# Row-tiled attention scores, attention beside the down projections, and a new start order in an encoder block

## Chip, cores, metric

One Trainium2 chip, eight NeuronCores, one sequence of the batch on each. Time is device microseconds of the slowest core. Some executions fall in a slower state, in which the cores of one die (0 to 3 or 4 to 7) show a lower granted clock; only fast runs are compared here.

## The reference, cut to what matters

```python
x = x + 0.5 * swiglu(rmsnorm(x), ffn1...)            # 1024 -> 2816 -> 1024
h = rmsnorm(x);  z = h @ w_in                        # q, k, v, two SGU halves, gates
y_att = chunked_rel_attention(q, k, v, rel_bias)     # 8 heads of 64; 64-frame chunks see 9 chunks
y_sgu = spatial_gating(gelu(z_sgu))                  # 128-frame blocks
x = x + (sig(g_att) * (y_att @ w_a) + sig(g_sgu) * (y_sgu @ w_s)) @ w_out
x = x + 0.5 * swiglu(rmsnorm(x), ffn2...)
out = rmsnorm(x)                                     # (8, 4096, 1024) float32
```

## The kernel before

Frames go in eight tiles of 512. Attention of tile t runs beside dense work of another tile, in turns: `interleave(main, attention, ...)` takes a piece of each. A block of keys (128) and two heads make one step: two score matmuls, one exp, one multiplication by exp(bias), and two steps later two value matmuls. Each head's query is padded with zeros to 128 rows (QZ).

```python
def scores(i):
    for h in range(2):
        matmul(bank(4 + h)[:, 0:n], lhsT=KT[:, hp, kcol:kcol + 128], rhs=QZ[:, hp, h, q0:q0 + n])
    act.activation(out=ee, in_=PS[2][...], func=Exp)
    dve.tensor_tensor(out=ee, in0=ee, in1=EB[...], op=mult)
def pv(i):
    for h in range(2):
        matmul(bank(6 + h)[:, q0:q0 + n], lhsT=VR[...], rhs=E[:, i % 2, h, 0:n], start=first, stop=last)
    ...            # after the last block: four copies of sums and values (VectorE, ScalarE)
def recip(i, j):   # VectorE, in halves; the sums are also added up on GpSimd (OKA)
# main of tile 1 and later: the whole FFN, gate/up first
interleave(ffn(t + 1, 0, True, hooks), attention(t), N_FFN - 6, n_att(t), 6)
# start: tile 1 lags tile 0 by one chunk of gate/up weights (last chunk of tile 1 later)
for n, f2 in enumerate(F2J):
    gu_chunk(0, f2, slot, ...)
    if prev is not None: gu_chunk(1, F2J[n - 1], prev, ...)
```

## Time and profile before

| | before |
|---|---|
| median of three runs | 2804.32 us |
| profiled run, slowest core | 2803.8 us |
| mean granted clock of the cores | 0.991 to 0.994 |
| TensorE busy; its share of the chain | 97%; 92% |

The prediction shows the lines. In them PE is TensorE's matmuls, PEld its weight loads, DVE VectorE, ACT ScalarE, POOL GpSimd and SP SyncE; L812 is a line of the kernel, and `ps` is PSUM, in banks of 512 columns. One tool is used throughout, its "loss": the length of a stretch less the work that TensorE did in it, with each weight load at 0.216 us (512 columns), attention and mixing by their columns.

### The profile page before, as it was taken

To read this page: it belongs to the slowest core of one execution; us is meant where nothing else is said; L and a number is where in the kernel's file an instruction comes from. 1 tells how busy PE (TensorE), PEld (TensorE's weight loads), DVE (VectorE), ACT (ScalarE), POOL (GpSimd) and SP (SyncE) were. 2 spreads that over 40 slices of the span, in tenths; PEclk is the share of its full clock that TensorE was granted. 3 is DMA by queue.
4 is the path that set the end of the run, shared out by engine and by line. 5 is a ranking of instruction groups with operands and counts; after the bars stand their busy time and mean duration, and the time that the engine had idled before them with its cause. 6 is when DMAs were issued, how large, how long until landed. Compare 5 with 4: busy or idle time off the path is not lost.

```text
span 2803.8 us, 38175 instructions; the slowest of 8 cores (2798.0 to 2803.8 us)
## 1 busy us (share of the span) xinstructions
PE 2705.7 (97%) x12775; PEld 1246.5 (44%) x13034; DVE 1318.1 (47%) x2007; ACT 897.7 (32%) x1348; POOL 406.5 (14%) x426
## 2 busy tenths in 40 slices
PE   6999899999999999999999999999999999999997
PEld 2443344444444444444444444444444444444443
DVE  4553744374433743347433464425644265466432
ACT  3322333243322423224232332323333242433221
POOL 2001311202121011111111111110110102100111
PEclk9999999999999999999999999999999999999998
DMA  8879899986798555984444634446344444333451
GB/s 150 175 134 178 181 208 176 186 260 153 194 184 218 174 148 160 227 239 143 141 160 143 201 130 143 151 146 204 131 150 144 158 154 139 142 130 128 141 195 69
DMA packets 113111, 461.94 MB, mean 165 GB/s; under 512 B 9352, under 2 KB 12424, under 8 KB 104848
## 3 DMA queue, kind: packets, MB, share of 16 engines
q1 hardware_dynamic: 89600, 365.68, 39.3%
q0 software_dynamic: 23168, 93.69, 21.7%
q8 instruction: 112, 1.84, 0.3%
q14 instruction: 87, 0.71, 0.1%
q10 hardware_dynamic: 144, 0.02, 0.0%
HBM read 488.03 MB, written 65.01 MB: 197 GB/s over the span
## 4 chain that ended last, share of the span: by engine, by line
PE 92%; DVE 3%; issue 2%; ACT 1%; DMA 1%; DVEq 0%; POOL 0%; ACTq 0%; POOLq 0%
PE ps L560 41%; PE ps L626 21%; PE ps L930 8%; PE ps L677 6%; PE ps L690 4%; PE ps L940 4%; PE ps L959 4%; PE ps L821 2%; PE ps L807 2%; DMA RING<-fsrc 1%; DVE TG L831 0%; DVE TG L829 0%; PE ps L764 0%; PE ps L501 0%; DVE TG L944 0%
## 5 line engine op out<-in xcount | busy, mean ns | idle before, releaser
L560 PE MATMUL ps<-XT,RING 128*128 128x512 bf16 x5501 | 1258.5, 381 | 38.3 <-DMA RING<-fsrc 14.7
L560 PEld LDWEIGHTS ps<-XT,RING 128*128 128x128 bf16 x5632 | 546.9, 98 | 674.0 <-issue 51.6
L626 PE MATMUL ps<-HT,RING 128*128 128x512 bf16 x2603 | 579.5, 379 | 2.8
L584 DVE TENSOR_TENSOR HT<-ps,TG 128x512 bf16<-128x512 f32 x332 | 227.9, 687 | 368.6 <-PE ps L560 318.8
L626 PEld LDWEIGHTS ps<-HT,RING 128*128 128x128 bf16 x2656 | 259.0, 98 | 309.2 <-issue 1.8
L490 POOL TENSOR_TENSOR ACC<-ACC,TG 128x512 f32<-128x512 f32 x174 | 224.1, 1288 | 994.0 <-ACT TG L487 992.9
L487 ACT ACTIVATE TG<-X 128x512 f32<-128x512 f32 x224 | 140.1, 627 | 476.6 <-DVE X L632 405.7
L632 DVE SCALAR_TENSOR_TENSOR X<-ps,X 128x512 f32<-128x512 f32 x128 | 87.8, 687 | 328.4 <-PE ps L626 324.4
L930 PE MATMUL ps<-XT,RING 128*128 128x512 bf16 x1003 | 239.7, 379 | 0.9
L811 ACT ACTIVATE E<-ps 128x1024 bf16<-128x1024 f32 (+1 forms) x240 | 168.7, 703 | 204.6 <-PE ps L807 187.3
L573 ACT ACTIVATE TG<-ps 128x512 f32<-128x512 f32 x154 | 92.0, 597 | 372.9 <-PE ps L560 367.4
L814 DVE TENSOR_TENSOR E<-E,EB 128x1024 bf16<-128x1024 bf16 (+1 forms) x240 | 152.7, 637 | 78.9 <-ACT E L811 77.6
L839 POOL TENSOR_TENSOR OKA<-OKA,TG 128x512 f32<-128x512 f32 x64 | 85.5, 1336 | 662.2 <-DVE TG L829 458.0
L677 PE MATMUL ps<-XT,RING 128*128 128x512 bf16 x752 | 167.5, 379 | 0.8
L569 DVE SCALAR_TENSOR_TENSOR TG<-TG,ps 128x512 f32<-128x512 f32 x154 | 103.6, 673 | 121.8 <-ACT TG L567 105.2
L944 DVE SCALAR_TENSOR_TENSOR TG<-TG,ps 128x512 f32<-128x512 f32 x128 | 87.1, 685 | 153.9 <-PE ps L940 126.2
L935 ACT ACTIVATE TG<-ps,BG 128x512 f32<-128x512 f32 x128 | 87.3, 687 | 213.1 <-PE ps L930 206.5
L930 PEld LDWEIGHTS ps<-XT,RING 128*128 128x128 bf16 x1024 | 99.7, 98 | 120.8 <-issue 3.1
L567 ACT ACTIVATE TG<-ps 128x512 f32<-128x512 f32 x154 | 91.9, 597 | 186.2 <-PE ps L560 183.2
L512 DVE SCALAR_TENSOR_TENSOR XT<-X,G,RSTD 128x512 bf16<-128x512 f32 x176 | 124.5, 744 | 36.5 <-ACT RSTD L505 36.5
L847 DVE RECIPROCAL TG<-TG 128x256 f32<-128x256 f32 x64 | 111.7, 1746 | 24.6 <-POOL OKA L839 24.5
L690 PE MATMUL ps<-RING,XT 128*128 128x512 bf16 x501 | 117.2, 385 | 5.6 <-DVE XT L512 4.6
(102 smaller groups left out, 1773.1 us busy)
## 6 DMA issues: line engine op xcount, KB each, us to landing
RING<-ffs SPq DMA_DIRECT2D x126, 1024.0 KB, 6.1
RING<-wds SPq DMA_DIRECT2D x93, 704.0 KB, 4.7
RING<-fsrc POOLq DMA_DIRECT2D x38, 1024.0 KB, 15.6
RING<-mgs SPq DMA_DIRECT2D x48, 768.0 KB, 4.8
RING<-wis SPq DMA_DIRECT2D x32, 1024.0 KB, 6.0
RING<-wd POOLq DMA_DIRECT2D x35, 704.0 KB, 17.0
ffs<-RING SPq DMA_DIRECT2D x22, 1024.0 KB, 15.5
out<-X SPq DMA_DIRECT2D x32, 512.0 KB, 6.2
```

The costliest lines, as they stand in the source:

```text
L487: p.add("act", lambda e: e.activation(out=buf[:], in_=src, func=AF.Square, scale=1.0 / 32.0), reads=[xres], writes=[bres])
L490: p.add(eng, lambda e: e.tensor_tensor(out=ACC[:], in0=ACC[:], in1=buf[:], op=ALU.add), reads=["ACC", bres], writes=["ACC"])
L512: p.add("dve", lambda e: e.scalar_tensor_tensor(out=dst, in0=src, scalar=G4[:, which * 8 + d:which * 8 + d + 1], in1=RSTD[:], op0=ALU.mult ...
L560: p.add("pe", lambda e: e.matmul(bank(b), lhsT=Wc[:, j * 1024 + kc * 128:j * 1024 + (kc + 1) * 128], rhs=xt[:, kc, :], start=(kc == 0), st ...
L584: p.add("dve", lambda e: e.tensor_tensor(out=dst, in0=bank(bu), in1=buf[:], op=ALU.mult), reads=[rb(bu), bres], writes=[dres])
L626: p.add("pe", lambda e, fc=fc, W=W, by=by, hap=hap: e.matmul(bank(by), lhsT=W[:, fc * 128:(fc + 1) * 128], rhs=hap, start=(fc == 0), stop= ...
L677: p.add("pe", lambda e, kc=kc, W=W, b=b, cc=cc: e.matmul(bank(b), lhsT=W[:, kc * 512 + cc * 128:kc * 512 + (cc + 1) * 128], rhs=XT[t % 2][ ...
L690: p.add("pe", lambda e, kc=kc, W=W, b=b, s=s: e.matmul(bank(b), lhsT=XT[t % 2][:, kc, s * 128:(s + 1) * 128], rhs=W[:, kc * 512:(kc + 1) * ...
L811: p.add("act", lambda e: e.activation(out=ee, in_=PS[2][:].rearrange("p (h c) -> p h c", h=2)[:, :, 0:n], func=AF.Exp), reads=[rb(4), rb(5 ...
L814: p.add("dve", lambda e: e.tensor_tensor(out=ee, in0=ee, in1=EB[:, 2 * hp:2 * hp + 2, u0:u0 + n], op=ALU.mult), reads=[("E", i % 2), ("EB" ...
L930: p.add("pe", lambda e, kc=kc, W=W, bgt=bgt, j=j: e.matmul(bank(bgt), lhsT=W[:, j * 1024 + kc * 128:j * 1024 + (kc + 1) * 128], rhs=XT[t % ...
L940: p.add("pe", lambda e, c4=c4, W=W, bbr=bbr, j=j, Y=Y: e.matmul(bank(bbr), lhsT=W[:, 2048 + j * 512 + c4 * 128:2048 + j * 512 + (c4 + 1) * ...
```

## The change

Intent: halve the score matmuls by running two heads in two row halves of the array; put attention only beside down projections, where ScalarE and VectorE have little else; replace slow reciprocals by exp(-log); start faster. The diff, cut to its core (left out: names of other buffers, weight layout and first loads, memsets moved to GpSimd, eight PSUM banks in the first gate/up stage, the order of the two branches in the merge, the fallback path):

```diff
-        E = sb("E", [128, 2, 2, T], BF16)
+        E = sb("E", [128, 4, 2, T], BF16)
-    bank(4 + h)[:, 0:n], lhsT=KT[:, hp, kcol:kcol + 128], rhs=QZ[:, hp, h, q0:q0 + n]
+    hs = slice(h * 64, (h + 1) * 64)        # two blocks of keys in a step, four banks
+    bank(2 + 2 * j + h)[:, q0:q1], lhsT=KT[hs, hp, kcol:kcol + 128], rhs=Q[hs, hp, q0:q1]
-    p.add("dve", ... e.reciprocal(out=r2[:, sl], in_=r2[:, sl]))
+    p.add("act", ... e.activation(out=r2[vs, :], in_=bank(6 + h)[ds, :], func=AF.Ln))
+    p.add("act", ... e.activation(out=r2[:], in_=r2[:], func=AF.Exp, scale=-1.0, accum_out=col))
+    for s in range(N + 1):                  # values half a step later
+        if s < N: scores(s); weigh(); yield
+        if s: pv(s - 1); yield
 ...
+    if narrow and fc in (5, 16): yield      # down projection in quarter pieces, two banks
-    main = ffn(t + 1, 0, True, ffn1_hooks(t + 1))
-    interleave(main, attention(t), N_FFN - 6, n_att(t), 6)
+    main = ffn(t + 1, 0, True, ffn1_hooks(t + 1), narrow=True)
+    interleave(main, attention(t), N_FFN + 16 - 3, n_att(t), 2 * NFC)
 ...
-    if prev is not None: yield from gu_chunk(1, F2J[n - 1], prev, ...)
+    if n == 1: yield from gu_chunk(1, F2J[0], prev, ..., first=0)
+    if 0 < n < len(F2J) - 1: yield from gu_chunk(1, f2, slot, ..., first=n)
+    second = down(1, 0, 0.5, Hooks(hk), ht_second, narrow=1)
+    for _ in range(4): next(second)         # ahead of the input projection
     win(0, {})
```

## The prediction

> **What bounds the kernel now.** I read the page first, its busy line and the chain that ended last.
> ```profile
> PE 2705.7 (97%) x12775; PEld 1246.5 (44%) x13034; DVE 1318.1 (47%) x2007; ACT 897.7 (32%) x1348; POOL 406.5 (14%) x426
> PE 92%; DVE 3%; issue 2%; ACT 1%; DMA 1%; DVEq 0%; POOL 0%; ACTq 0%; POOLq 0%
> ```
> The chain is TensorE for 92% of the span; VectorE, the next, is busy for 47%. So time falls only if TensorE gets less work or loses fewer microseconds. A busy share of 97% does not tell these two apart, so I looked at the spacing of matmuls in the timeline (start, length, engine).
> ```profile
> 562.37 0.59 PE L807 MATMUL ps<-QZ,KT 128*128 128x512 bf16 x2
> ...
> 564.86 1.89 PE L560 MATMUL ps<-XT,RING 128*128 128x512 bf16 x8
> ```
> One matmul is shown 0.38 us long, but eight take 1.89, so they start (1.89 - 0.38) / 7 = 0.216 us apart, and the score pair, 0.59 - 0.38 = 0.21, too. That is the price of 512 columns; a weight load (98 ns) hides beside it.
>
> Work, from the kernel's loops: a tile of 512 frames has 1056 matmuls in the two FFNs, 160 in the input projection and 256 in the merge, 1472 in all; eight tiles are 11,776 x 0.216 = 2541 us. Attention of a full tile: 20,480 score columns and as many for values, each 40 x 0.216 = 8.6 us. Tile 0 has half, so 7.5 x 8.6 = 65 us each. Spatial mixing and the norm sums are some 22. Sum 2693 us; about 110 us of the span are losses.
>
> Where are they? In stretches of the span I count weight loads (second "x", no record missing there), price them as above, and subtract from the length. Columns: stretch, length, busy (count) of PE, PEld, DVE, ACT, POOL, then clock.
> ```profile
> 0.00:61.00 61.00, 35.53 (x121) 12.97 (x124) 28.36 (x43) 20.00 (x29) 21.00 (x30) 0.92 0.94 166
> 61.00:177.00 116.00, 115.42 (x528) 52.59 (x538) 71.05 (x116) 35.03 (x46) 6.82 (x11) 1.00 0.78 156
> 177.00:192.00 15.00, 9.38 (x33) 3.60 (x32) 11.52 (x18) 1.89 (x3) 1.59 (x3) 0.77 0.37 63
> 224.00:250.00 26.00, 20.00 (x76) 7.90 (x76) 11.03 (x17) 8.84 (x11) 1.06 (x2) 0.87 0.99 203
> 280.00:340.00 60.00, 48.84 (x253) 22.26 (x256) 43.19 (x60) 20.50 (x31) 20.39 (x19) 0.94 0.87 182
> 588.00:928.00 340.00, 336.56 (x1605) 156.23 (x1636) 156.55 (x239) 111.78 (x170) 59.11 (x64) 1.00 0.83 198
> ```
> Start: 61 - 124 x 0.216 = 34 us lost. The next 116 us: none. At 177: 15 - 32 x 0.216 = 8. At 224, where the input projection of tile 0 waits for its norm: 26 - 76 x 0.216 = 9.6. At 280, attention of tile 0: 64 loads are attention (8.6 us), 32 mixing (1.8), 160 dense (34.5), so 60 - 45 = 15. The stretch from 588 is one steady tile: 1476 dense loads (318.5), attention 17.4, mixing 1.8, so only 2.3 lost of 340. Summing the other steady tiles the same way gives 14.5 for six, the last attention 6.6, and about 21 at the end, where no matmul follows. Most losses thus lie before 340 us. The waits of TensorE name their causes (us in total, times, longest):
> ```profile
> PE ps L821 <- DVE TG L831: 15.3, 18, 3.8
> PE ps L560 <- DMA RING<-fsrc: 14.7, 4, 10.4
> PE ps L560 <- DVE HT L584: 10.9, 3, 5.6
> PE ps L807 <- ACT E L811: 5.8, 5, 1.4
> PE ps L690 <- DVE XT L512: 4.6, 3, 3.7
> ```
> The first is a value matmul that needs the bank the previous head pair's copies still read; the second the first weights; the third, around 178 us, VectorE clearing QZ.
>
> **What the Trainium skill says.** "TensorEngine Tiling (Array Packing)", Tiling Modes / Key Properties: two 64-row tiles work in parallel, but changing the tiling mode "drains the TensorE". No row tile runs here yet; the mixing matmuls (64 output columns) are column tiles and show both:
> ```profile
> 454.14 5.13 PE L560 MATMUL ps<-XT,RING 128*128 128x512 bf16 x23 [0.16 <-issue]
> 459.20 0.41 PE L764 MATMUL ps<-WST,HT 128*64 128x128 bf16 x8
> 459.54 0.82 PE L560 MATMUL ps<-XT,RING 128*128 128x512 bf16 x3
> ```
> Inside, starts are (0.41 - 0.22) / 7 = 0.027 us apart, half of 0.054 for 128 columns. The last dense matmul before starts at 454.14 + 5.13 - 0.38 = 458.89 and the next at 459.54: 0.65, less 0.216 for that one and 8 x 0.027 = 0.22 for the block: 0.21 us for going in and out.
> "TensorE: Matmul & The Clock Gate", Part 1: after idling, the array runs at half rate until busy for about 3.4 us. Agrees: after the wait at 178 us the mean clock of 177 to 192 is 0.77, so long waits cost more than their length.
> "SBUF — State Buffer", Terms, shared port pair: VectorE and GpSimd exclude one another there. Agrees: the 768-wide weighting took 1.25 us at 588.8 beside a GpSimd sum, 0.56 at 591.0 alone.
> "ScalarE: Activation LUTs", What ACT_TABLE_LOAD costs: 1283 ns a set. The trace has 1283 at each Ln of a norm, and none at the Exp after it, so the new Ln should cost one load a tile, after which the norm needs none.
>
> **The change part by part.**
> 1. Row-tiled scores. Both heads' 64-row matmuls run together: half of 65 us goes, -32. But each score step is a block of its own tiling: 12 per full tile, 8 in tile 0, 92 in all x 0.21 (estimate from the column case) = +19. Net -13.
> 2. Attention beside the down projection, values half a step later. A tile's down matmuls are 176 x 0.216 = 38 us, cut into 32 pieces of 1.19; 25 half steps go between the last 29. A step (two halves) then lasts 2.3 x 1.19 for dense work and about 1.3 for its own, 4.0 us; its two exps take 2 x 1.02 plus the sums that they now accumulate (for which I have no duration; 0.1 each assumed). Per head pair: ScalarE 5 exps (5.6 us), two Ln and one Exp (1.9), up to two squares (1.3), 8.8 of 12.4. VectorE: weightings 152.9 / 7.5 / 4 = 5.1, copies 1.4, product 0.8, down results 1.3, 8.6. Neither is the bound on average. What goes: in a steady tile 1.6 of the 2.3 lost (waits at the head pairs). But an exp can stand behind a square, this behind a down result, this behind weightings on VectorE: I allow 1.5 back. So about 0 per steady tile, -3 in the last, whose mixing no longer shares the stretch.
> 3. Reciprocals. VectorE loses 111.7 us (64 x 1.746), GpSimd 85.5 of sums; ScalarE replaces two copies (0.59 each) by two Ln and adds an Exp, 32 x 0.63 = 20 us. All off TensorE's path except in tile 0, whose waits behind it (4 us at 306, 1.2 to 1.6 elsewhere) make up the 15. There I leave 7: mixing now shares two banks with the down results. -8.
> 4. Start. Tile 0 computes chunks 0 and 1, then tile 1 both, so the third chunk of weights is needed one chunk (32 x 0.216 = 6.9 us) later; the first loads are contiguous and chunk 1 no longer competes with chunk 0. -12 of 34.
> 5. No QZ to clear (3.47 us of VectorE), VR (1.76) to GpSimd: nearly all of the 8 at 177, -7.5.
> 6. Four quarter pieces (22 matmuls, 4.75 us) of the down projection ahead of the input projection. But the seventh of them reads HT of the last chunk, whose product ends at 241.4, so most of that wait stays: -3.
> 7. Contiguous gate and up weights, the branch order in the merge, and the larger E: no wait in the steady stretch is on them; 0.
> Sum: -13 - 3 - 8 - 12 - 7.5 - 3 = -46.5. I round it to -50, since a step that was timed with quarter pieces may lose less than the 1.5 us a tile that I allowed.
>
> **The rivals.** (a) ScalarE becomes the wait: exps wait behind Ln, Exp and squares, and scores for banks 2 to 5. For it: 71% mean load in coupled in-order queues, and scores that can be issued again only when both exps have read their four banks. Against it: four weight buffers and half a step of distance. At 4 us a tile, +17 on the sum, about 2771. (b) Switching tilings costs more than in the column case, or the two heads do not overlap fully: at 0.4 us a block the row tiling gives nothing back, +18; without overlap +32 more, near 2800. (c) All goes as intended: no stalls beside down, switch 0.15, start and tile 0 at half of their losses: about 2728. (d) The first loads are bound by DMA (0.94 busy in the first 61 us) whatever the order: +8.
>
> **Range and chances.** The middle is 2804 - 50 = 2754. 8 in 10: 2728 (c) to 2784 (a with part of b). Two per cent is 2748, a little below the middle, so faster by over 2% has 0.42, within 2% 0.56; slower by 2% would need b in full plus stalls, 0.02.
>
> **What would show it.** Row tiling: score starts of two heads almost together, a pair of 512 in 0.22, and about 0.2 us extra at each block. Step 2: a steady tile at 338 to 339 us; if TensorE waits on exps (E) in the down stretches, rival a. Step 3: no wait on the copies above 2 us in tile 0. Step 4: dense work without gaps from about 50 us. Step 5: no wait near 178. The prediction is wrong if the steady tile is under 336 or over 342 us, or if the loss of the first 61 us falls by under 6 or over 20.

## The result, and the profile after

Fast runs of the changed kernel lie between 2788.09 and 2791.17 us (median 2789.7), those of the kernel before at 2804.2 and 2804.3. The ratio is 0.9948, 95% interval 0.9924 to 0.9972: 0.5% faster, where 1.8% was the middle of the forecast and 2784 us the edge of the range. (A ratio is the mean time of one kernel's fast runs over that of the other's of the same rounds, so not quite the ratio of the medians.)

The page of the changed kernel, the same two lines as before:
```profile
PE 2702.4 (97%) x13034; PEld 1209.5 (43%) x13034; DVE 1183.2 (42%) x1940; ACT 910.7 (33%) x1466; POOL 311.5 (11%) x356
PE 88%; DMA 5%; DVE 3%; ACT 2%; issue 2%; DVEq 0%; SPq 0%; POOL 0%; ACTq 0%; POOLq 0%
```
The second line needs care: most of the 5% of DMA is a chain that ends in one wait of this core, see run 4. TensorE is still the bound. Its waits (us in total, times, longest):
```profile
PE ps L812 <- ACT E L818: 14.0, 16, 1.3
PE ps L547 <- DMA RING<-fsrc: 10.6, 1, 10.6
PE ps L547 <- DVE XT L504: 7.6, 6, 2.9
PE ps L618 <- DVE HT L571: 7.1, 2, 5.0
PE ps L547 <- DMA RING<-ffs: 6.2, 1, 6.2
PE ps L618 <- DVE X L624: 5.9, 4, 2.9
...
PE ps L835 <- ACT TG L844: 2.8, 12, 0.2
```
Most waits named in the prediction are gone or shrunk (the 15.3 on the head pairs' copies is 2.8 on the Ln), but that of the scores for exps has grown from 5.8 to 14.0 us (L812), and others are new: L618, the down projection, waits 7.1 for products of the gate and up stage and 5.9 for X, and the first gate/up stage 7.6 for its scaled input XT. Stretches as in the prediction (length, PE, PEld, DVE, ACT, POOL, clock, DMA):
```profile
0.00:61.00 61.00, 41.94 (x170) 16.77 (x171) 31.94 (x51) 21.89 (x32) 15.29 (x23) 0.97 0.94 185
160.00:184.00 24.00, 19.85 (x85) 8.26 (x84) 12.88 (x24) 3.78 (x6) 2.11 (x4) 0.93 0.57 99
215.00:244.00 29.00, 23.16 (x97) 9.75 (x96) 10.89 (x17) 10.48 (x14) 2.09 (x4) 0.88 0.87 182
955.00:1294.40 339.40, 336.88 (x1640) 151.71 (x1636) 141.23 (x231) 113.44 (x184) 40.69 (x44) 1.00 0.66 187
```
Start: 61 - 171 x 0.216 = 24 us lost (was 34). The next two rows: 24 - 84 x 0.216 = 6 and 29 - 96 x 0.216 = 8. The last is a steady tile: 339.4, before 340.0. I repeated this count on all eight cores, with both heads' scores priced in full, so that overlap shows as a gain of its own. Means over the cores, us lost:

| stretch | before | after | change | predicted |
|---|---|---|---|---|
| to 61: start | 32.2 | 25.2 | -7.0 | -12 |
| 61 to 200: constants, end of first gate/up | 8.2 | 6.8 | -1.4 | -7.5 |
| 200 to 255: norm before input projection | 9.6 | 8.6 | -1.0 | -3 |
| 255 to 340: attention of tile 0 | 14.5 | 8.0 | -6.5 | -8.5 |
| 340 to 2440: steady tiles | 14.4 | 11.8 | -2.6 | -11 |
| from 2440: last attention, last tile, end | 28.2 | 28.2 | 0.0 | -5 |
| sum | 107.1 | 88.6 | -18.5 | -47 |

The predicted column spreads its first step (-13) over the tiles. Every row gave less than forecast. The largest part is missing in the steady tiles: I had 338.1 us in mind (340.0 - 1.8 of row tiling), they take 339.36. This period, from the first score matmul of a tile to that of the next, is the same to 0.02 us for all steady tiles of a core, so it is the sharpest gauge here.

That the two heads overlap shows in TensorE's timeline:
```profile
950.62 2.54 PE L618 MATMUL ps<-HT,RING 128*128 128x512 bf16 x11
953.09 0.60 PE L812 MATMUL ps<-Q,KT 64*128 64x512 bf16 x4
953.62 1.25 PE L618 MATMUL ps<-HT,RING 128*128 128x512 bf16 x5
```
Four score matmuls of 512 columns start within 0.60 - 0.38 = 0.22 us, in two pairs. From the last dense start (950.62 + 2.54 - 0.38 = 952.78) to the next (953.62) it is 0.84, less 0.216 and 0.43 for the two pairs: 0.19 us for the two switches, 0.21 predicted. So step 1 was sized well, and the wait lies behind it:
```profile
974.22 0.69 DVE L853 TENSOR_TENSOR YA<-TG 128x512 bf16<-128x512 f32 x1
...
974.94 0.69 DVE L624 SCALAR_TENSOR_TENSOR X<-ps,X 128x512 f32<-128x512 f32 x1
975.73 0.63 ACT L474 ACTIVATE TG<-X 128x512 f32<-128x512 f32 x1 [2.48 <-DVE X L624]
976.26 1.01 ACT L818 ACTIVATE E<-ps 128x1024 bf16<-128x1024 f32 x1
...
977.50 0.61 PE L812 MATMUL ps<-Q,KT 64*128 64x512 bf16 x4 [1.15 <-ACT E L818]
```
Read it upward. The scores at 977.50 waited for an exp to empty their banks. That exp could start only at 976.26, although its scores were done at about 973.0. ScalarE had been idle for 2.48 us, because next in its queue was a square of the next norm, waiting for X. X is VectorE's down result, which stood behind four weightings and the product YA. The down result itself was ready at about 972.7 (its last matmuls start at 971.22 and end 1.46 later). Two queues served in order thus turned a free ScalarE into a wait of TensorE. This is rival (a) of the prediction.

### The profile page after: what moved, and what is told of

The parts are those of the page before. It is cut to its first block, busy times and chain, and to the rows that moved or that the text cites. A ratio compares the mean times of both kernels' runs of the same rounds, so it can differ in the third digit from the quotient of the medians.

```text
span 2786.6 us, 38337 instructions; the slowest of 8 cores (2777.5 to 2786.6 us)
## 1 busy us (share of the span) xinstructions
PE 2702.4 (97%) x13034; PEld 1209.5 (43%) x13034; DVE 1183.2 (42%) x1940; ACT 910.7 (33%) x1466; POOL 311.5 (11%) x356
## 4 chain that ended last, share of the span: by engine, by line
PE 88%; DMA 5%; DVE 3%; ACT 2%; issue 2%; DVEq 0%; SPq 0%; POOL 0%; ACTq 0%; POOLq 0%
PE ps L547 40%; PE ps L618 19%; PE ps L930 8%; PE ps L671 6%; PE ps L684 4%; PE ps L940 4%; PE ps L959 4%; PE ps L835 2%; DMA ffs<-RING 2%; PE ps L812 1%; ACT E L818 1%; DMA RING<-fsrc 1%; DMA RING<-wd 1%; DMA RING<-ffs 1%; DMA X<-xT 1%
## 5 line engine op out<-in xcount | busy, mean ns | idle before, releaser
L547 PE MATMUL ps<-XT,RING 128*128 128x512 bf16 x5632 | 1232.5, 380 | 25.4 <-DMA RING<-fsrc 10.6
L547 PEld LDWEIGHTS ps<-XT,RING 128*128 128x128 bf16 x5632 | 547.6, 98 | 691.8 <-issue 41.3
L618 PE MATMUL ps<-HT,RING 128*128 128x512 bf16 x2656 | 607.6, 380 | 9.2 <-DVE HT L571 7.1
L618 PEld LDWEIGHTS ps<-HT,RING 128*128 128x128 bf16 x2656 | 252.9, 98 | 317.4 <-issue 36.3
L930 PE MATMUL ps<-XT,RING 128*128 128x512 bf16 x1024 | 241.9, 379 | 2.8 <-ACT TG L935 1.6
L823 DVE TENSOR_TENSOR E<-E,EB 128x1024 bf16<-128x1024 bf16 (+1 forms) x240 | 120.1, 504 | 168.3 <-ACT E L818 157.7
L818 ACT ACTIVATE E<-ps 128x1024 bf16<-128x1024 f32 (+3 forms) x156 | 152.5, 983 | 67.2 <-PE ps L812 62.8
L671 PE MATMUL ps<-XT,RING 128*128 128x512 bf16 x768 | 168.4, 379 | 0.0
L930 PEld LDWEIGHTS ps<-XT,RING 128*128 128x128 bf16 x1024 | 98.5, 98 | 127.1 <-issue 12.9
L671 PEld LDWEIGHTS ps<-XT,RING 128*128 128x128 bf16 x768 | 75.2, 98 | 90.6
L959 PE MATMUL ps<-HT,RING 128*128 128x512 bf16 x448 | 99.0, 379 | 2.1 <-DVE HT L949 2.1
```

The lines of the kernel that those rows point to most:

```text
L547: p.add("pe", lambda e: e.matmul(bank(b), lhsT=Wc[:, kc * 512 + j * 128:kc * 512 + (j + 1) * 128], rhs=xt[:, kc, :], start=(kc == 0), stop ...
L618: p.add("pe", lambda e, fc=fc, W=W, by=by, hap=hap: e.matmul(bank(by), lhsT=W[:, fc * 128:(fc + 1) * 128], rhs=hap, start=(fc == 0), stop= ...
L671: p.add("pe", lambda e, kc=kc, W=W, b=b, cc=cc: e.matmul(bank(b), lhsT=W[:, kc * 512 + cc * 128:kc * 512 + (cc + 1) * 128], rhs=XT[t % 2][ ...
L818: p.add("act", lambda e, j=j, sl=sl, qa=qa, col=ok_col(): e.activation(out=E[:, sl, :, qa:T], in_=PS[1 + j][:].rearrange("p (h c) -> p h c ...
L823: p.add("dve", lambda e, sl=sl, q0=q0, q1=q1, u0=u0: e.tensor_tensor(out=E[:, sl, :, q0:q1], in0=E[:, sl, :, q0:q1], in1=EB[:, 2 * hp:2 * ...
L930: p.add("pe", lambda e, kc=kc, W=W, bgt=bgt, j=j: e.matmul(bank(bgt), lhsT=W[:, j * 1024 + kc * 128:j * 1024 + (kc + 1) * 128], rhs=XT[t % ...
```

## The experiments

Every kernel was timed in five rounds against the kernel before. Times below are medians of the fast runs. The first four ran on one chip, the next four on a second, the last four on a third. On each, the runs of the kernel before that count as fast fall into two groups, 2802 to 2806 us and 2819 to 2822 us (two cores at a clock of about 0.982); on the third chip five of six are of the second. So I compare times and tile periods, not ratios. The changed kernel has 2789.7 us and a steady tile of 339.36; it was not timed again on these chips, so a difference of one or two microseconds in the times shows nothing, while the steady tile of runs 3, 4, 5 and 7, which leave it alone, is 339.36 on both of their chips.

**1. Both heads in one row half** (`e_same_rows`; wrong result):
```diff
-                                hs = slice(h * 64, (h + 1) * 64)
+                                hs = slice(0, 64)
```

> Wrong result on purpose: in the changed kernel both heads' score matmuls read the rows of the first head (partitions 0 to 63), so the tiling of 64 rows and its switches stay, but two heads can no longer overlap. Theory (the overlap was had in full, as the trace of the changed kernel shows, where four score matmuls of 512 start within 0.22 us): the second head's 32 us come back, so about 2790 + 31 = 2821 us. Rival (the heads overlapped only in part, which is why the gain was small): under 2806.

Measured: 2811.2 us, steady tile 342.34. Four score matmuls of 512 columns now take 1.03 us in the trace (at 955.57 us), where it was 0.60. The overlap is worth 21.5 us (2.98 a tile), not 31: waits for exps fell from 14.0 to 9.6 and those of the values for the Ln went away. I read this as slower scores leaving ScalarE more time. The direction is the theory's, and the rival (under 2806) is out; the size says that part of what overlap frees was waited away.

**2. Scores over all rows** (`e_full_rows`; wrong result):
```diff
-                                hs = slice(h * 64, (h + 1) * 64)
+                                hs = slice(0, 128)
```

> Wrong result on purpose: the score matmuls use all 128 rows (both heads summed), so there is neither overlap nor a switch of tiling. Theory (a block costs 0.19 us for its two switches, 92 blocks, 17 us; the overlap is worth 31): 2790 + 31 - 17 = 2804 us, so the row tiling was worth 14 us net, much as predicted (13). Rival (switches cost about as much as the overlap brings): 2790 or less.

Measured: 2799.2 us, steady tile 340.67. The row tiling is worth 9.5 us net in the changed kernel, 1.31 a tile. The rival is out, but the theory's 14 us are not had either. Runs 1 and 2 differ by the switching alone: 1.67 us a tile, 0.14 a block, net of waits for exps, which are 9.6 us in run 1 and 12.3 in run 2.

**3. Start order of before** (`e_order_undone`):
```diff
-                n_dense[0] = 8
+                n_dense[0] = 6
-                by_k = first == 0 or (first == 1 and t == 0)
+                by_k = first == 0
-                    if n == 1: ... gu_chunk(1, F2J[0], prev, ..., first=0)
-                    if 0 < n < len(F2J) - 1: ... gu_chunk(1, f2, slot, ..., first=n)
+                    if prev is not None: ... gu_chunk(1, F2J[n - 1], prev, ..., first=n - 1)
```

> The changed kernel with the start order of before: tile 1 lags tile 0 by one chunk, six banks, only the first chunk contraction-slice by slice. Theory (what the start wins is given back twice: the last chunk's product is read at once by the down projection, 6 us at 170 to 177, and the weights of the third FFN pass, bound by DMA until about 595 us, do not come earlier): the first 61 us lose about 7 more than in the changed kernel (31 in place of 24), the waits at 170 and 589 us shrink or go, and the time is within 4 us of 2790. Rival (the start's 10 us are kept to the end): 2797 to 2800.

Measured: 2783.4 us, 6 faster than with the new order, where the theory had allowed 4. Its stretches:
```profile
0.00:61.00 61.00, 40.07 (x147) 15.29 (x150) 31.04 (x49) 21.46 (x31) 14.41 (x22) 0.92 0.92 173
160.00:184.00 24.00, 23.89 (x111) 10.89 (x112) 14.23 (x26) 4.41 (x7) 5.14 (x8) 1.00 0.66 105
```
The start loses 61 - 150 x 0.216 = 28.6 on this core (mean 28.6, against 25.2), but 160 to 184 loses nothing: 112 loads fill 24 us. In the new order the down projection follows at once on the last chunk of tile 0. It waits there twice, for a bank that the gate and up stage still holds and for the product of that chunk, its seventh and eighth operand; these are lines of the changed kernel:
```profile
172.13 3.15 PE L618 MATMUL ps<-HT,RING 128*128 128x512 bf16 x7 [2.08 <-DVE TG L563]
...
177.35 3.83 PE L618 MATMUL ps<-HT,RING 128*128 128x512 bf16 x17 [2.07 <-DVE HT L571]
```
In the old order a chunk of tile 1 (6.9 us) lies between. So the first half of the theory holds: what the order wins at the start it gives back 100 us later, and more. (The run undoes the order, the eight banks and the slicing of the second chunk together, so it does not tell these apart.) The rest of the kernel differs by less than 1 us. The second half, on the weights at 589 us, is not shown: see run 4.

**4. Later write-back of four weight chunks** (`e_wb_late`):
```diff
-    at = {("ffs", 0, f2): int(n < 4) for n, f2 in enumerate(F2J)}
+    at = {("ffs", 0, f2): 2 * (n < 4) for n, f2 in enumerate(F2J)}
```

> The changed kernel with the write-back of four converted weight chunks (4 MB) moved from the second use (about 510 to 580 us, where the DMA engines are busy 1.0 of the time) to the third (about 850 to 900 us, 0.4 busy). Theory (the wait of 6.2 us for the weights at 589 us, with 1.5 us of half clock after it, is DMA backlog of that stretch): it goes, 2790 - 7 = 2783 us. Rival (the wait has another cause, as the order of one queue, or comes back at the later conversion): 2788 to 2792.

Measured: 2788.7 us. A miss. The wait at 589 us is gone on all cores, and yet nothing is gained beyond a microsecond. Looking again at the changed kernel, only core 5, which happened to be the slowest in the profile, has that wait: between 560 and 608 us it loses 7.6 us, the other seven 0.7 at most. I had read a cause of the kernel's time from a single core. (Between 850 and 900 us the DMA engines are also busier than expected, 0.69 of the time in the changed kernel and not 0.4.)

**5. Last chunk's slices last in the down projection** (`e_fc_order`):
```diff
+                order = list(range(NFC))
+                if i == 0 and t < 2:
+                    order = [fc for fc in order if fc not in (6, 7)] + [6, 7]
-                n_dense[0] = 4            # at the end of the first gate/up stage
```

> The changed kernel, with the down projections of the first FFN of tiles 0 and 1 contracting the slices of the last weight chunk (6 and 7) last, and eight banks kept during the first of them. Theory (the chunk order of the start moved a wait: the down projection reads the last chunk's product at once, 6.8 us lost at 170 to 177 and 5 of the 8.6 at 215 to 244, means over the cores): the loss up to 200 us falls from 32 to about 26 and that from 200 to 255 from 8.6 to about 6, so 2789 - 8 = 2781 us. Rival (the later stages give it back, as DMA does at 589 us on one core): 2786 to 2790.

Measured: 2781.7 us, 8 us gained, as expected. The two stretches:
```profile
160.00:184.00 24.00, 21.41 (x95) 9.45 (x94) 15.56 (x28) 4.40 (x7) 2.11 (x4) 0.96 0.68 120
215.00:244.00 29.00, 26.19 (x121) 11.65 (x120) 11.24 (x17) 11.16 (x15) 2.11 (x4) 1.00 0.93 186
```
24 - 94 x 0.216 = 3.7 and 29 - 120 x 0.216 = 3.1 are lost, where it was 6 and 8. The clock of the second row is 1.00, in the changed kernel 0.88: the long wait had also cost half-rate time (after it, from 229 to 233 us, weight loads start 0.43 us apart there, in place of 0.216).

**6. Three moves against waits beside attention** (`e_no_stalls`). The squares move by 11 matmuls, half of one output of the down projection:
```diff
-                    add_hook(hk, D1 + 2 * d + 1, P(nsq, t, d))                  # squares
+                    add_hook(hk, min(D1 + 2 * d + 2, D1 + 15), P(nsq, t, d))
-                return 2 * len(att_steps(t)) + 1
+                return 2 * len(att_steps(t)) + 1 + (t > 0)
+                        if s == 0 and t: yield        # after scores(0)
+                if t == 0: dense_bank()               # mixing skips a bank
```

> The changed kernel with three moves that touch only waits beside attention: the squares of the next norm are issued half a piece of the down projection later, so that no exp stands behind a square that waits for VectorE; one idle half step after the first score step; and in tile 0 mixing skips a bank, so that two down results don't follow each other in one bank. Theory (what the row tiling wins in a steady tile is lost to TensorE's waits for exps, 1.31 + 0.77 us a tile, and in tile 0 to 5.9 us for X): the waits on E fall from 14 to under 4 us, those of down on X from 5.9 to about 2, so 2789 - 13 = 2776 us, a steady tile at 337.3 in place of 339.4. Rival (ScalarE's queue is simply too full, and the waits move to other steps): waits on E stay above 9 us, 2785 or more.

Measured: 2767.8 us, 22 less, more than expected; steady tile 336.59. The waits:
```profile
PE ps L814 <- ACT E L820: 2.5, 3, 1.3
...
PE ps L837 <- DVE TG L848: 0.6, 2, 0.4
```
Exps 2.5 in place of 14.0, down results waiting for X gone from the list, the values' wait 0.6 in place of 2.8. The attention of tile 0 loses 3.6 us, not 8.0. ScalarE does the same work as before (busy 911.7 us against 910.7), so it was never too full: when each piece is issued made the waits, not how much there is. The rival falls. The steady tile also closes the account: 340.0 less 1.8 for the row tiling and 1.6 for the old waits, with nothing given back, is 336.6.

**7. Spreading the last pieces** (`e_tail`):
```diff
-                    interleave(last_ffn, attention(t + 1), N_FFN + 16 - 8, ...)
+                    interleave(last_ffn, attention(t + 1), N_FFN + 16 - 10, ...)
+                    next(last_ffn); next(last_ffn)      # ahead of the last merge
-                    next(last_ffn)                      # ahead of the last norm sum
+                    next(last_ffn); next(last_ffn)
```

> The changed kernel with the eight quarter pieces left of the last FFN's down projection spread out: two ahead of the last merge, two (in place of one) ahead of the last norm sum, four ... six in all after the attention. Theory (quarter pieces, in place of halves, left too little dense work to cover the last merge's first tanh, 1.6 us, and the norm sum, 1.5 us): those two waits go, some comes back as waits on E in the denser attention, 2789 - 2 = 2787 us. Rival: no change, or slower.

Measured: 2791.0 us, not faster. The wait for the norm sum fell (5.3 to 3.8 in the list of waits), the waits on exps rose (14.0 to 14.5), and the loss from 2440 us on did not fall (it rose by 1 us). Three waits after the last attention are named in the trace (1.6 for a tanh, 1.5 for the norm sum, 0.6 for X), and moving pieces won little of them back. The trace of the changed kernel shows a loss that no list of waits names. This is its last merge (line 935 is the tanh that reads the gate's bank):
```profile
2583.22 1.89 PE L930 MATMUL ps<-XT,RING 128*128 128x512 bf16 x8 [1.56 <-ACT TG L935]
...
2585.21 0.69 ACT L935 ACTIVATE TG<-ps,BG 128x512 f32<-128x512 f32 x1 [2.13 <-PE ps L930]
2586.04 1.89 PE L930 MATMUL ps<-XT,RING 128*128 128x512 bf16 x8
2588.86 1.89 PE L930 MATMUL ps<-XT,RING 128*128 128x512 bf16 x8
```
Its gates start 2.82 to 2.87 us apart, in the merge of the tile before 2.59. From the first branch to the last it takes 44.1 us on every core, in the kernel before 38.9: 5.2 us lost. The kernel says why it may be so: the narrow down projection sets `n_dense` to two banks and gives the four back only with its last output, and here two of its outputs are still to come when the merge runs. So each gate needs the bank that the last tanh is still reading, and the first of them waits for a table load of 1.28 us (at 2581.10), too. Run 7 leaves this as it is (43.9 us). No run gives the merge its four banks, so this is read and not tested.

**8. All together** (`e_best`): the edits of runs 4, 5, 6 and 7.

> All of the above together, with the write-backs one use later as well. If the parts are independent: -8 - 13 - 2 - 1, about 2766 us, 1.4% below the kernel before. If the gains share a bound (DMA backlog near 590 us, or ScalarE): 2775 or more.

Measured: 2758.2 us (three fast runs, 2757.6 to 2760.1; ratio to the kernel before 0.983, interval 0.9785 to 0.9875). The measured parts add up (-1, -8, -22 and +1 from 2789.7 are 2760); run 6 alone had brought 8 us more than expected.

**9. The squares alone** (`e_squares`):
```diff
-                    add_hook(hk, D1 + 2 * d + 1, P(nsq, t, d))
+                    add_hook(hk, min(D1 + 2 * d + 2, D1 + 15), P(nsq, t, d))
```

> The changed kernel with only the squares of the next norm issued half a piece of the down projection later. Theory (ScalarE's in-order queue: an exp stands behind a square, which stands behind a down result on VectorE): the wait of 1.31 us a tile for an exp and the two waits of 0.23 for the Ln go, about 1.8 to 2.1 us a tile, 2789 - 13 = 2776 us. Rival (it was the idle half step that helped): under 5 us.

**10. The idle half step alone** (`e_gap`):
```diff
-                return 2 * len(att_steps(t)) + 1
+                return 2 * len(att_steps(t)) + 1 + (t > 0)
+                        if s == 0 and t: yield        # after scores(0)
```

> The changed kernel with only the idle half step after the first score step of tiles 1 to 7. Theory (the second score step comes one piece after the first, when two exps of 1.0 us are not through): the wait of 0.77 us a tile goes, 2789 - 5 = 2784 us. Rival (the wait only moves on, as the exps behind it come no earlier): 2788 or more.

Measured in runs 9 and 10: 2777.3 us and a tile of 337.35 (on the undisturbed die) for the squares; 2786.0 us and 338.47 for the idle half step. Of 2.77 us a tile the squares bring 2.01, the idle half step 0.89. Both theories hold by the tile period. The times of run 10 alone, 2784.1 to 2788.3, would not have told its theory from its rival (2788).

**11. Scores over all rows, without the waits** (`e_quiet_full`; wrong result): the edits of runs 6 and 2.

> Wrong result on purpose: the kernel without the waits beside attention (2768 us), with score matmuls over all 128 rows, so neither overlap nor switch. Theory (the row tiling is worth 31 - 17 = 14 us where TensorE does not wait for exps; in the changed kernel, where the slower scores hid part of the waits, it was worth 10): 2768 + 14 = 2782 us. Rival (it is worth 10 in both): 2778 or less.

Measured: 2782.1 us, steady tile 338.33, against 336.59: the row tiling is worth 14.3 us, 1.74 a tile, where TensorE does not wait; 9.5 and 1.31 where it does. The prediction had 13 and 1.8.

**12. All together without the spread** (`e_best2`): run 8 less the edit of run 7.

> All the moves that helped, without the spread of the last pieces, which cost 1 to 2 us alone: about 2757 us, if that loss adds up here too; 2759 or more if it does not.

Measured: 2759.7 us (three fast runs, 2759.5 to 2760.7), no different from run 8 by what two chips can show. That the spread costs 1 to 2 us did not add up here.

## Why the prediction was wrong

The bound was named rightly: TensorE, with all that ends its waits. The chance that it gave "within 2%" (0.56) was the larger one, but the forecast of 2754 missed by 36 us, and the range, 2728 to 2784, by 6. Step by step, by its own numbers (one product is off: 11,776 x 0.216 is 2544, not 2541, on which nothing rests):

1. *Row tiling, -13.* Right in mechanism and in size: 0.19 us a block against 0.21, full overlap, 14.3 us net in run 11. In the changed kernel a third of it was waited away (9.5, run 2).
2. *"I allow 1.5 back. So about 0 per steady tile."* This is the step that failed most, 8 us over the steady tiles. The mechanism, an exp behind a square behind a down result, was in the text; its size was not. Removing these waits took 2.77 us from every steady tile (runs 6, 9, 10), nearly twice the allowance, and some 22 us from the whole with tile 0. And I then rounded the sum to -50 on the hope that the tuning had avoided them: a reason not from the profile. ScalarE's mean load (8.8 of 12.4 us) that I gave in the rival's favour was not the point: its load is unchanged in run 6. What counts is the order in the queue at the time.
3. *Reciprocals, tile 0: -8.* Nearly right: -6.5, with the shared banks that I foresaw (5.9 us of waits for X, gone when mixing skips a bank). One reading behind it was wrong: the new Ln did not spare the norm its table load. The norms have 31 loads as before, the Ln adds 6, and the merge has 15 in place of 7, since its tanh changes the tables between the Ln of attention and that of the norm.
4. *Start, -12.* -7.0. The third chunk is needed later, as said, but the trace of the changed kernel shows TensorE waiting for the scaled input of tile 1 instead (7.6 us, XT). That this is what took the rest is read from the list of waits and was not tested: the cause of these 5 us stays open.
5. *"No QZ to clear ... nearly all of the 8 at 177, -7.5."* -1.4. The VectorE memset and its wait did go. (Of the 10.9 us that I put down to it only 5.6 were at 178 us; 5.3 lay in the first 61 us.) But the new order of chunks (step 4) put the down projection right behind the chunk that it reads seventh. I saw exactly this for the second down projection in step 6, and did not look for it at the first. Runs 3 and 5 show it: with the old order the stretch loses nothing, with the slices last 3.6.
6. *Pieces ahead of the input projection, -3.* -1.0, for the reason given there; run 5 gets nearly 5 us more from the same stretch.
7. *The last tile, -3.* The stretch from 2440 us gained nothing. From the first score to the last value of the last attention the loss fell by 6.9 us, more than forecast; from there to the last matmul it rose by as much, 5.2 of it in the last merge, where two PSUM banks are left in use (run 7; read, not tested). The prediction had no term for this side of its narrow down projection.

Of the 28 us that the table has missing, steps 4 and 5 are 11, the steady tiles 8, the end 5, step 6 and tile 0 4. The rest of the 36 is the rounding to -50 (3.5), and that the rows are means over the cores of one run (-18.5) while the median time of the slowest core fell by 14.6. Rival (b), costly switches, was not at work; rival (d), a start bound by DMA, was not tested (the DMA engines are busy 0.94 of the first 61 us in both kernels). The test in the prediction, "wrong if the steady tile is under 336 or over 342", was too wide to catch a failure of 1.3 us a tile.

The experiments also show what the change held: with the waits moved out of the way it gives 2758 us, 1.7% below the kernel before (2804.7 on that chip). That this lies near the forecast of 2754 does not bear the forecast out: runs 5 and 6 are further changes.

## What to carry to other kernels

When work is moved beside other work, draw the queues of the helper engines in order and ask what stands ahead of the instruction that frees a buffer; a mean load of 70% says nothing of it, and putting a small square 11 matmuls later was worth 12 us here (run 9). When the order of a producer is changed, look which of its results the consumer reads first, and let it read the newest last. Where a stage is given fewer buffers, look which later stage still runs with them. And count a wait on all cores before giving it a cause.

## What the Trainium skill lacked or had wrong

- "TensorEngine Tiling (Array Packing)", Key Properties, says that a change of tiling mode drains the TensorE but gives no cost: here 0.19 us for going in and out of a block of row tiles by the trace, 0.14 by the difference of runs 1 and 2 (1.67 us for 12 blocks, net of fewer waits). Its "Up to 2×" for two row tiles (Overview, Theoretical Speedup) is had in full inside a block: four matmuls of 512 columns start within 0.22 us.
- "ScalarE: Activation LUTs", What it computes, names the accumulator output without a cost. The timeline of ScalarE in the changed kernel, below, shows it as an instruction of its own, 0.19 us long, most of it beside the exps on either side: the next exp starts 1.01 us after the one before. The sum, for which I had assumed 0.1 us, costs no more than that.
- "TensorE: Matmul & The Clock Gate", Part 1 (its paragraph on engine queue depths), says that ScalarE and VectorE are strict first-in first-out. No page that I read says what this does to a neighbour: here 2.77 us of a 339 us tile, with ScalarE busy for a third of the time.

```profile
953.58 1.02 ACT L818 ACTIVATE E<-ps 128x1024 bf16<-128x1024 f32 x1 [3.78 <-PE ps L812]
954.50 0.19 ACT L818 ACTIVATION_READ_ACCUMULATOR E<-ps 128x1 f32 x1
954.59 1.01 ACT L818 ACTIVATE E<-ps 128x1024 bf16<-128x1024 f32 x1
```
